# Two attention layers: where the compression weights are loaded and split, the order of the stick-breaking projections, and how small vectors reach 128 partitions

## The chip, the cores and the metric

The kernel runs on one core of one Trainium2 chip. The metric is the device time of one execution in microseconds. The engines are named as the profile names them: PE is TensorE, DVE is VectorE, ACT is ScalarE, POOL is GpSimd, SP is SyncE, which here only issues transfers. PEclk is TensorE's granted clock as a share of the full 2.4 GHz.

## What is computed

A sequence of 256 tokens of width 1024 goes through a first block and then through two hybrid layers. Each of them is a feed-forward part, a mixer and another feed-forward part. The first block's mixer has forgetting attention and differential attention; the hybrid mixer has three branches. Cut to what touches the change:

```python
def token_mixer(h, w_in, fox_forget_b, lam_q1, lam_k1, lam_q2, lam_k2, subln_g, w_out, layer):
    proj = h @ w_in
    ...
    log_f = log_sigmoid(fgate + fox_forget_b)
    ...
    lam = exp(sum(lam_q1 * lam_k1)) - exp(sum(lam_q2 * lam_k2)) + lam_init
    diff_o = a1 - lam * a2
    diff_o = rms_norm(diff_o, subln_g) * (1.0 - lam_init)

def hybrid_mixer(h, w_in, w_gate, nsa_q_norm, nsa_k_norm, nsa_cmp_pe, nsa_cmp_w1, nsa_cmp_w2, ...):
    (sb_q, sb_k, sb_v, nq, nkc, nvc, nks, nvs, nkw, nvw, ngate,
     dq, dk, dv, iq, ik, iw) = split(h @ w_in)
    o_a = stick_breaking_attention(sb_q, sb_k, sb_v)          # 4 heads of 64
    o_b = nsa_attention(nq, nkc, nvc, nks, nvs, nkw, nvw, ngate, ...)
    o_c = dsa_attention(dq, dk, dv, iq, ik, iw, dsa_q_norm, dsa_k_norm, ...)
    g_a, g_b, g_c = split(sigmoid(h @ w_gate), 3)
    merged = g_a * (o_a @ w_br_a) + g_b * (o_b @ w_br_b) + g_c * (o_c @ w_br_c)
    return merged @ w_out

def nsa_compress(x, pe, w1, w2):      # w1: 2048 x 128, twice a layer (keys, values)
    ...
    return silu(flat @ w1) @ w2
```

The small vectors are gains of 64 numbers (nsa_q_norm, three of nsa_k_norm, dsa_q_norm, dsa_k_norm), and in the first mixer subln_g (128), the forget bias (8) and four lambda vectors (64 each).

## The kernel before

All products of activations with weights are made in fp32r, in three matmuls each (mm3, lines 250 to 254): a weight tile of 128x1024 numbers is loaded by SP into a buffer raw (fetch, four buffers), ACT copies it to hi (line 238), DVE subtracts to get lo (line 239), and PE multiplies hi with the high part of the activations, lo with the high part, and hi with the low part. The name after the underscore in a row is the section of the program in which the tile was made: ffn, m (first mixer), and in the hybrid mixer sb (stick-breaking projections), ckv (compressed, selected and windowed keys and values), nq (nsa's queries), ix (the index), dsaq (dsa's queries, keys, values), top, cmp (compression), nsa, dsa, gate, br (branch weights), wo.

The program is written section by section; a scheduler then orders the instructions of each engine, and an engine works through its own queue strictly in that order. The queue matters in four places here.

- The stick-breaking projection. self.proj runs 256 value columns, evacuated by ACT as sbv, then 512 columns of queries and keys, evacuated by ACT in two halves as tok_sb (line 512 through scaled), which PE transposes (tp_sb, line 558) before the scores at_sb (line 906). With skew, the first token tile's matmuls start ahead of the second's.
- The small vectors. small_load issues a transfer from POOL's software queue, which reads one vector for all 128 partitions (partition_broadcast, small_gain).
- The compression weights w1. Eight loads of 256 KB (line 1033) are issued behind nq's weight loads into buffers that are free there, and split_w1 makes their hi (line 1098, ACT) and lo (line 1099, DVE), 128x512 at a time. It is called in section cmp, but the scheduler puts the splits among the steps of ix and dsaq.
- The gate's products (mm_gate, 288 matmuls in a layer) need only the normalised activations and their own weights. The scheduler spreads them as filler over dsaq, cmp, nsa and dsa, up to the branch products mm_br.

In dsaq, the evacuated projection is normalised, multiplied by the gain gA and rotated by a chain of small DVE steps (lines 549, 531 to 539, 552, 521 to 524), to tok_dsaq; PE then transposes it (tp_dsaq, line 1084).

Of the kernel before, what the change touches and what calls it, by code (L numbers as in the profile page):

```python
# [117 lines left out]
class K:  # L118
    def __init__(self, ctx, tc, d):
        self.tc, self.nc, self.d = tc, tc.nc, d  # L120
        nc = self.nc
# [128 lines left out]
    def mm3(self, out, xh, xl, wh, wl, first, last):  # L250
# [242 lines left out]
        with self.tc.issue_after(self.lastpow):  # L493
            self.nc.gpsimd.dma_start(out=out, in_=in_)

    def small_gain(self, pool, g, reps, tag):

        n = g.shape[0]
        t = self.tile(pool, [P, reps, n], tag)
        self.small_load(out=t, in_=bass.AP(tensor=g.tensor, offset=g.offset,  # L500
                                                    ap=[[0, P], [0, reps], [1, n]]))
        return t
# [142 lines left out]
    def mixer1(self, nxt):  # L645
        nc, tc, d = self.nc, self.tc, self.d
        self.sec = "m1"
        self.exp_ln_tables()
        xs = self.prenorms(d["mix_pre_g"][0])
        w = d["w_in"][0]  # L650
        with tc.tile_pool(name="mix1", bufs=1) as mp:
            T = lambda shape, tag, bufs=1, dt=F32: self.tile(mp, shape, tag, dt, bufs)
# [32 lines left out]
            with tc.issue_after(self.lastlo):  # L685
                post = self.gain(d["mix_post_g"][0], mp)
                sel = T([96, 8 * P], "sel", 1, BF)
                self.small_load(out=sel, in_=d["const_sel"])
                gsub = self.small_gain(mp, d["diff_subln_g"][0], 4, "gsub")
                nc.vector.tensor_scalar(out=gsub, in0=gsub, scalar1=0.8, scalar2=None, op0=OP.mult)  # L690
                fb = self.small_gain(mp, d["fox_forget_b"][0], 1, "fb")[:, 0]
                lv = T([P, 4, 64], "lv")
# [148 lines left out]
    def mixer2(self, l, nxt):  # L841
# [7 lines left out]
        with ExitStack() as outer:  # L849
# [27 lines left out]
            kn = G("nsa_k_norm")
            gS = T([P, 4, 64], "gS")
            self.small_load(out=gS[:, 0:2], in_=self.rep(kn[1], 2))
            self.small_load(out=gS[:, 2:4], in_=self.rep(kn[2], 2))  # L880
            gC = T([P, 64], "gC")
            self.small_load(out=gC, in_=kn[0].partition_broadcast(P))
            w2 = T([P, 2, 64], "w2")
            self.small_load(out=w2, in_=G("nsa_cmp_w2").rearrange("v h d -> h v d"))
            pe = T([32, P], "pe")
            self.small_load(out=pe, in_=G("nsa_cmp_pe").rearrange("v (m r) d -> (v m) (r d)", r=2))
# [142 lines left out]
            last = T([P, 8, P], "dq")  # L1029
            raws += [last[:, :4], last[:, 4:]]  # L1030
            for i, r in enumerate(raws):
                with tc.issue_after(self.lastraw):
                    nc.sync.dma_start(out=r, in_=G("nsa_cmp_w1")[i // 4, 512 * (i % 4):512 * (i % 4) + 512]
                                      .rearrange("(m p) h -> p m h", p=P))
            homes = [L([P, 4, 2, P], "gl", 6, F32R) for _ in range(6)]
            homes.append(self.tile(self.spool, [P, 4, 2, P], "xg", F32R, bufs=1))
            homes += [T([P, 2, 2, P], "sp", 2, F32R) for _ in range(2)]
            w1 = [u[:, m] for u in homes for m in range(u.shape[1])]

            gA = T([P, 5, 64], "gA")  # L1040
            self.small_load(out=gA[:, 0:4], in_=self.rep(G("dsa_q_norm"), 4))
            self.small_load(out=gA[:, 4:5], in_=self.rep(G("dsa_k_norm"), 1))
# [50 lines left out]
            def split_w1(i):
                for k in range(0, 4, 4 if i < 7 else 2):
                    u = homes[i + k // 2]
                    r = raws[i][:, k:k + u.shape[1]]
                    with tc.issue_after(self.lasthi):
                        nc.scalar.copy(u[:, :, 0], r)
                    nc.vector.tensor_sub(u[:, :, 1], r, u[:, :, 0].bitcast(F32))  # L1099
# [354 lines left out]
```

## Time and profile before

| | |
|---|---|
| time, median of 3 runs | 1785.98 us (1784.88 to 1786.46) |
| the profiled execution's own time | 1785.48 us |
| its span, first to last instruction | 1783.7 us |
| mean granted clock of PE | 0.994 |
| PE, DVE, ACT, POOL busy | 98%, 63%, 52%, 2% of the span |
| chain that ended last, by engine | PE 86%, DVE 7%, ACT 4%, DMA 3%, issue 1% |
| q0 (small vectors, issued by POOL) | 848 packets, 1.48 MB, 1.5% of 16 engines' span |
| q1 (weights, issued by SP) | 150400 packets, 301.61 MB, 54.4% |

All times are of one core. The profile is of one execution, whose own time stands beside its span. Layer 0's mixer begins at about 710 us and layer 1's at about 1339 us, 629 us later, and the two look alike; the first mixer begins at about 204 us.

### The profile page before, as it was taken

The page shows a single profiled execution, that of the slowest core. Times are in us where ns is not written, and L with a number is a line of the kernel's source. Part 1 is how long each engine was busy: PE and PEld are TensorE (multiplying, and loading weights), DVE is VectorE, ACT ScalarE, POOL GpSimd, SP SyncE. Part 2 cuts the span into 40 slices and gives each one's busy share as a digit, 9 for nine tenths or more (in the row PEclk, how much of TensorE's full clock was granted, in tenths as well). Part 3 has the DMA queues.
Part 4 walks back from the last instruction along what each step waited for, and adds up shares of the span by engine and source line. Part 5 has one row for each costly group of instructions (what it writes and reads, how often), then busy time and mean ns, then how long its engine had stood idle before and what let it go on. Part 6 is the DMA issues. An engine that isn't in the chain of part 4 may idle for free.

```text
span 1783.7 us, 22942 instructions
## 1 busy us (share of the span) xinstructions
PE 1743.5 (98%) x8461; PEld 1433.3 (80%) x8461; DVE 1115.8 (63%) x1801; ACT 931.6 (52%) x1445; POOL 44.2 (2%) x81
## 2 busy tenths in 40 slices
PE   8999989999999999989999999999999899999999
PEld 6888777888878888867887888888888777878887
DVE  5555577555565556697867555555555978675553
ACT  5444467544454444666655444444445756554442
POOL 0000200000000000000000000000001000000000
PEclk9999999999999999999999999999999999999999
DMA  8665754466556656734245665566567353356653
GB/s 279 185 187 191 187 144 142 136 185 187 188 172 206 185 184 203 179 117 141 86 129 187 199 184 184 189 194 185 188 205 176 114 147 91 110 165 207 185 187 130
DMA packets 151952, 305.08 MB, mean 171 GB/s; under 512 B 10440, under 2 KB 42224, under 8 KB 151840
## 3 DMA queue, kind: packets, MB, share of 16 engines
q1 hardware_dynamic: 150400, 301.61, 54.4%
q0 software_dynamic: 848, 1.48, 1.5%
q8 instruction: 67, 1.10, 0.3%
q10 hardware_dynamic: 592, 0.53, 0.1%
q14 instruction: 45, 0.37, 0.1%
HBM read 302.53 MB, written 1.05 MB: 170 GB/s over the span
## 4 chain that ended last, share of the span: by engine, by line
PE 86%; DVE 7%; ACT 4%; DMA 3%; issue 1%; POOL 0%; SPq 0%; DVEq 0%; ACTq 0%; POOLq 0%
PE mm_ffn L254 10%; PE mm_ffn L253 10%; PE mm_ffn L252 10%; PE at_ffn L254 9%; PE at_ffn L252 9%; PE at_ffn L253 9%; PE mm_gate L253 2%; PE mm_gate L254 2%; PE mm_gate L252 2%; PE tp_ffn L290 1%; DMA raw_ckv<-in_w_in_dram 1%; PE po_ffn L290 1%; PE mm_m L254 1%; PE mm_m L252 1%; PE mm_m L253 1%
## 5 line engine op out<-in xcount | busy, mean ns | idle before, releaser
L239 DVE TENSOR_TENSOR lo_ffn<-raw_ffn,hi_ffn 128x1024 fp32r<-128x1024 f32 x392 | 478.1, 1225 | 452.9 <-ACT hi_ffn L238 451.7
L238 ACT CAST hi_ffn<-raw_ffn 128x1024 fp32r<-128x1024 f32 x392 | 411.3, 1054 | 498.4 <-PE at_ffn L254 307.3
L252 PE MATMUL mm_ffn<-hi_ffn,xh_ffn 128*128 128x512 f32 x288 | 112.3, 391 | 2.9 <-ACT hi_ffn L345 1.9
L253 PE MATMUL mm_ffn<-lo_ffn,xh_ffn 128*128 128x512 f32 x288 | 112.3, 391 | 1.0 <-DVE lo_ffn L347 1.0
L254 PE MATMUL mm_ffn<-hi_ffn,xl_ffn 128*128 128x512 f32 x288 | 112.2, 390 | 0.0
L253 PE MATMUL mm_ffn<-lo_ffn,ah_ffn 128*128 128x512 f32 x264 | 103.8, 393 | 0.0
L252 PE MATMUL mm_ffn<-hi_ffn,ah_ffn 128*128 128x512 f32 x264 | 103.3, 391 | 0.0
L253 PE MATMUL at_ffn<-lo_ffn,ah_ffn 128*128 128x512 f32 x264 | 103.1, 390 | 0.0
L254 PE MATMUL at_ffn<-hi_ffn,al_ffn 128*128 128x512 f32 x264 | 102.9, 390 | 0.0
L252 PE MATMUL at_ffn<-hi_ffn,ah_ffn 128*128 128x512 f32 x264 | 102.8, 389 | 0.0
L254 PE MATMUL mm_ffn<-hi_ffn,al_ffn 128*128 128x512 f32 x264 | 102.8, 389 | 0.0
L252 PE MATMUL at_ffn<-hi_ffn,xh_ffn 128*128 128x512 f32 x240 | 94.5, 394 | 0.0
L254 PE MATMUL at_ffn<-hi_ffn,xl_ffn 128*128 128x512 f32 x240 | 93.5, 390 | 0.0
L253 PE MATMUL at_ffn<-lo_ffn,xh_ffn 128*128 128x512 f32 x240 | 93.4, 389 | 0.0
L252 PE MATMUL mm_gate<-hi_gate,xh_ffn 128*128 128x512 f32 x192 | 79.3, 415 | 4.6 <-DVE xg_nq L1099 4.6
L253 PE MATMUL mm_gate<-lo_gate,xh_ffn 128*128 128x512 f32 x192 | 80.1, 417 | 1.6 <-DVE lo_gate L239 1.6
L254 PE MATMUL mm_gate<-hi_gate,xl_ffn 128*128 128x512 f32 x192 | 80.6, 420 | 0.0
L253 PE MATMUL mm_ffn<-lo_ffn,xh_wo 128*128 128x512 f32 x192 | 74.9, 390 | 0.0
L254 PE MATMUL mm_ffn<-hi_ffn,xl_wo 128*128 128x512 f32 x192 | 74.8, 389 | 0.0
L252 PE MATMUL mm_ffn<-hi_ffn,xh_wo 128*128 128x512 f32 x192 | 74.7, 389 | 0.0
L252 PEld LDWEIGHTS mm_ffn<-hi_ffn,xh_ffn 128*128 128x128 f32 x288 | 54.1, 188 | 14.9 <-ACT hi_ffn L345 2.6
L253 PEld LDWEIGHTS mm_ffn<-lo_ffn,xh_ffn 128*128 128x128 f32 x288 | 54.1, 188 | 12.7 <-DVE lo_ffn L347 1.6
(624 smaller groups left out, 4003.3 us busy)
## 6 DMA issues: line engine op xcount, KB each, us to landing
raw_ffn<-in_ffn_w_gu_dram SPq DMA_DIRECT2D x160, 512.0 KB, 3.7
raw_ffn<-in_ffn_w_down_dram SPq DMA_DIRECT2D x132, 512.0 KB, 3.2
raw_gate<-in_w_gate_dram SPq DMA_DIRECT2D x48, 512.0 KB, 3.7
raw_ffn<-in_ffn_w_gate_dram SPq DMA_DIRECT2D x40, 512.0 KB, 4.3
raw_ffn<-in_ffn_w_up_dram SPq DMA_DIRECT2D x40, 512.0 KB, 3.7
raw_m<-in_w_in_dram SPq DMA_DIRECT2D x22, 512.0 KB, 4.0
raw_ffn<-in_ffn_w_gu_dram SPq DMA_DIRECT2D x32, 256.0 KB, 3.2
raw_wo<-in_w_out_dram SPq DMA_DIRECT2D x16, 512.0 KB, 3.5
```

Source lines behind the costliest of these rows:

```text
L238: self.lasthi = nc.scalar.copy(hi, raw).ins
L239: self.lastlo = nc.vector.tensor_sub(lo, raw, hi.bitcast(F32)).ins
L252: nc.tensor.matmul(out, xh, wh, start=first, stop=False)
L253: nc.tensor.matmul(out, xh, wl, start=False, stop=False)
L254: self.lastmm = nc.tensor.matmul(out, xl, wh, start=False, stop=last).ins
L290: nc.tensor.transpose(p[:, i], src[:, i * P:(i + 1) * P], self.ident)
```

## The change

It has three parts.

1. The eight loads of w1 are issued right behind the hybrid mixer's first eight weight loads, into buffers ob0, qS and ob1. load and split are called from wtiles: with each weight tile that the projection takes, one more entry of self.extra is run. Seven of the eight splits (now lines 900 and 901) thus stand between the first weight tiles' splits; the eighth stays in cmp.
2. Queries and keys (512 columns, with skew) are projected first, the 256 value columns behind them.
3. The small vectors are loaded to one partition (rows), in a row of the tile junk, and spread by one matmul with a column of -1 into PSUM; ACT copies them out with a scale of -1 (in the first mixer, -0.8 for the gain that DVE scaled before).

```diff
@@ wtiles
             hi, lo = self.load(w, r0 + k0 * P, m, c0, n)
+            if self.extra:
+                self.extra.pop(0)()
             yield k0, [(hi[:, k], lo[:, k]) for k in range(m)]
@@
-    def small_gain(self, pool, g, reps, tag):
...
+    def rows(self, vecs):
+
+        n = sum(v.shape[-1] * (v.shape[0] if len(v.shape) > 1 else 1) for v in vecs)
+        row = self.tile(self.spool, [1, n], "junk", bufs=1)
+        c = 0
+        for v in vecs:
+            v = v if len(v.shape) == 1 else v.rearrange("a b -> (a b)")
+            self.small_load(out=row[:, c:c + v.shape[0]], in_=v[None, :])
+            c += v.shape[0]
+        p = self.tp([P, n])
+        self.nc.tensor.matmul(p, self.neg1[:1].bitcast(F32), row, start=True, stop=True)
+        return p
@@ the first mixer
-                gsub = self.small_gain(mp, d["diff_subln_g"][0], 4, "gsub")
-                nc.vector.tensor_scalar(out=gsub, in0=gsub, scalar1=0.8, scalar2=None, op0=OP.mult)
-                fb = self.small_gain(mp, d["fox_forget_b"][0], 1, "fb")[:, 0]
+                r = self.rows([d["diff_subln_g"][0], d["fox_forget_b"][0]]
+                              + [d["diff_lambda_" + n][0] for n in ("q1", "k1", "q2", "k2")])
+                gsub = T([P, 4, P], "gsub")
+                nc.scalar.activation(gsub, r[:, None, :P].to_broadcast([P, 4, P]), AF.Copy, scale=-0.8)
+                fb = T([P, 8], "fb")
+                self.scaled(fb, r[:, P:P + 8], -1.0)
                 lv = T([P, 4, 64], "lv")
-                for i, n in enumerate(("q1", "k1", "q2", "k2")):
-                    self.small_load(out=lv[:, i], in_=d["diff_lambda_" + n][0].partition_broadcast(P))
+                self.scaled(lv, r[:, P + 8:].rearrange("p (i d) -> p i d", d=64), -1.0)
@@ the hybrid mixer
+            raws = []
+            for u in (L([P, 8, P], "ob0"), T([P, 16, P], "qS"), L([P, 8, P], "ob1")):
+                raws += [u[:, i:i + 4] for i in range(0, u.shape[1], 4)]
...
+            def extra(k):
+                if k < 8:
+                    load_w1(k)
+                if 0 <= k - 3 < 7:
+                    split_w1(k - 3)
+            self.extra = [lambda k=k: extra(k) for k in range(10)]
+
             self.sec = "sb"
-
-            sbv = [T([P, 256], f"sbv{t}") for t in range(2)]
-            self.proj(xs, w, 512, 256, lambda t, ps: self.scaled(sbv[t], ps, xs[t][2]), skew=True)
-            gQ = T([P, 64], "gQ")
-            self.small_load(out=gQ, in_=G("nsa_q_norm").partition_broadcast(P))
...
-            self.proj(xs, w, 0, 512, sb_evac)
+            self.proj(xs, w, 0, 512, sb_evac, skew=True)
+            sbv = [T([P, 256], f"sbv{t}") for t in range(2)]
+            self.proj(xs, w, 512, 256, lambda t, ps: self.scaled(sbv[t], ps, xs[t][2]))
+            r = self.rows([G("nsa_q_norm"), G("nsa_k_norm"), G("dsa_q_norm"), G("dsa_k_norm")])
...
-            raws = [L([P, 8, P], "ob1")]
-            raws = [raws[0][:, :4], raws[0][:, 4:]]
-            raws += [T([P, 4, P], tag, bufs) for tag, bufs in (("rl", 2), ("rl", 2), ("P", 3), ("P", 3))]
...
@@ cmp
             for v in range(2):
-                for i in range(4):
-                    split_w1(4 * v + i)
+                if v == 1:
+                    split_w1(7)
```

The scheduler decides what this does to each engine's queue. The first place is SP's queue at the start of layer 0's mixer, where raw_sb and raw_ckv are loads of mixer weights and raw_nq those of nsa's queries. Before, from the seventh mixer load on, and then at the end of nq's loads:

```order
L223 DMA raw_ckv_6166<-in_w_in_dram 128x2x512
L223 DMA raw_ckv_6184<-in_w_in_dram 128x2x512
L281 DMA gain_wo_8515<-in_ffn_norm_dram 128x1024
L223 DMA raw_ckv_6202<-in_w_in_dram 128x2x512
...
L223 DMA raw_nq_6481<-in_w_in_dram 128x2x512
L223 DMA raw_nq_6499<-in_w_in_dram 128x2x512
L1033 DMA ob_nq_6579<-in_nsa_cmp_w_2_dram 128x4x128 x2
L1033 DMA dq_nq_6584<-in_nsa_cmp_w_2_dram 128x4x128 x2
L1033 DMA P_nq_6582<-in_nsa_cmp_w_2_dram 128x4x128
L223 DMA raw_ix_6610<-in_w_in_dram 128x3x296
L1033 DMA P_nq_6583<-in_nsa_cmp_w_2_dram 128x4x128
```

Now, from the same load on:

```order
L224 DMA raw_ckv_6202<-in_w_in_dram 128x2x512
L224 DMA raw_ckv_6223<-in_w_in_dram 128x2x512
L891 DMA ob_pn_5876<-in_nsa_cmp_w_2_dram 128x4x128 x2
L891 DMA qS_pn_5877<-in_nsa_cmp_w_2_dram 128x4x128 x4
L891 DMA ob_pn_5878<-in_nsa_cmp_w_2_dram 128x4x128 x2
L284 DMA gain_wo_8523<-in_ffn_norm_dram 128x1024
L224 DMA raw_ckv_6244<-in_w_in_dram 128x2x512
L224 DMA raw_ckv_6264<-in_w_in_dram 128x2x512
```

The eight loads of nsa_cmp_w1 have moved ahead of gain_wo and of the third raw_ckv.

The second place is ACT's queue in the same stretch; L238 (now L239) makes hi of a weight tile, tok_sb are the evacuated queries and keys. Before:

```order
L238 CAST hi_sb_6007<-raw_sb_6005 128x1024
L238 CAST hi_ckv_6168<-raw_ckv_6166 128x1024
L238 CAST hi_ckv_6186<-raw_ckv_6184 128x1024
L238 CAST hi_ckv_6204<-raw_ckv_6202 128x1024
L512 ACTIVATE tok_sb_6023<-mm_sb_5949,rsv_pn_5866 128x256
L512 ACTIVATE tok_sb_6023<-mm_sb_5949,rs_ffn_5780 128x256
L512 ACTIVATE tok_sb_6032<-mm_sb_5950,rsv_pn_5866 128x256
```

Now, from the first split of w1 (L900) on:

```order
L294 CAST xh_ffn_5839<-po_ffn_5850 128x512
L900 CAST gl_pn_5879<-ob_pn_5876 128x4x128
L520 ACTIVATE tok_sb_5967<-mm_sb_5887,rsv_pn_5871 128x256
L520 ACTIVATE tok_sb_5967<-mm_sb_5887,rs_ffn_5785 128x256
L239 CAST hi_sb_5991<-raw_sb_5989 128x1024
L900 CAST gl_pn_5880<-ob_pn_5876 128x4x128
L239 CAST hi_sb_6024<-raw_sb_6022 128x1024
L900 CAST gl_pn_5881<-qS_pn_5877 128x4x128
L239 CAST hi_ckv_6204<-raw_ckv_6202 128x1024
L900 CAST gl_pn_5882<-qS_pn_5877 128x4x128
L520 ACTIVATE tok_sb_5976<-mm_sb_5888,rsv_pn_5871 128x256
L520 ACTIVATE tok_sb_5976<-mm_sb_5888,rs_ffn_5860 128x256
```

tok_sb stood behind the third hi_ckv; it stands behind hi_sb of the value weights now, with three splits of w1 around it, and the third hi_ckv behind all of it.

The third place is the end of dsaq in layer 0. On DVE, where gl and xg are homes of the split w1, L549 (now L557) begins tok_dsaq and lo_gate is the low part of a gate weight tile. Before:

```order
L1099 TENSOR_TENSOR gl_nq_6595<-rl_nq_6580,gl_nq_6595 128x4x128
L1062 COPY zs_ix_6606<-tp_ix_6704 128x128
L1099 TENSOR_TENSOR gl_nq_6596<-rl_nq_6581,gl_nq_6596 128x4x128
L1099 TENSOR_TENSOR gl_nq_6597<-P_nq_6582,gl_nq_6597 128x4x128
L549 SCALAR_TENSOR_TENSOR tok_dsaq_6789<-mm_dsaq_6715,rs_ffn_5780,gA_nq_6602 128x320
L531 TENSOR_REDUCE sm_dsaq_6793<-junk_dsaq_6790 128x5
L1099 TENSOR_TENSOR gl_nq_6598<-P_nq_6583,gl_nq_6598 128x4x128
L1099 TENSOR_TENSOR xg_nq_6599<-dq_nq_6584,xg_nq_6599 128x4x128
```

Now:

```order
L1088 COPY zs_ix_6626<-tp_ix_6707 128x128
L901 TENSOR_TENSOR sp_cmp_6999<-ob_pn_5878,sp_cmp_6999 128x2x128
L901 TENSOR_TENSOR sp_cmp_7000<-ob_pn_5878,sp_cmp_7000 128x2x128
L240 TENSOR_TENSOR lo_gate_7712<-raw_gate_7709,hi_gate_7711 128x1024
L1088 COPY zs_ix_6626<-tp_ix_6724 128x128
L557 SCALAR_TENSOR_TENSOR tok_dsaq_6809<-mm_dsaq_6735,rs_ffn_5785,gA_sb_6070 128x320
L539 TENSOR_REDUCE sm_dsaq_6813<-junk_dsaq_6810 128x5
L240 TENSOR_TENSOR lo_gate_7730<-raw_gate_7727,hi_gate_7729 128x1024
```

The splits of w1, but for the last, are gone from here, and the first lo_gate stands ahead of tok_dsaq. On PE, at the same place, behind the last product of dsaq. Before:

```order
L254 MATMUL mm_dsaq_6716<-hi_dsaq_6773,xl_ffn_5835 128x408
L252 MATMUL mm_gate_7699<-hi_gate_7703,xh_ffn_5759 128x512
L252 MATMUL mm_gate_7700<-hi_gate_7703,xh_ffn_5834 128x512
L1084 MATMUL tp_dsaq_6814<-ident,tok_dsaq_6789 128x128 x2
L1084 MATMUL tp_dsaq_6814<-ident,kd_dsaq_6812 128x128
L253 MATMUL mm_gate_7699<-lo_gate_7704,xh_ffn_5759 128x512
```

Now:

```order
L257 MATMUL mm_dsaq_6736<-hi_dsaq_6793,xl_ffn_5840 128x408
L255 MATMUL mm_gate_7707<-hi_gate_7711,xh_ffn_5764 128x512
L256 MATMUL mm_gate_7707<-lo_gate_7712,xh_ffn_5764 128x512
L257 MATMUL mm_gate_7707<-hi_gate_7711,xl_ffn_5765 128x512
...
L256 MATMUL mm_gate_7708<-lo_gate_7730,xh_ffn_5839 128x512
L257 MATMUL mm_gate_7708<-hi_gate_7729,xl_ffn_5840 128x512
L1110 MATMUL tp_dsaq_6834<-ident,tok_dsaq_6809 128x128 x2
```

Two gate matmuls stood between the last mm_dsaq and the first tp_dsaq; 24 stand there now (rows 3458 to 3481 of PE's order).

## Rows read from the trace of the kernel before

**Rows 1.** Page, part 1: busy us (share of the span) x instructions, by engine.

```profile
PE 1743.5 (98%) x8461; PEld 1433.3 (80%) x8461; DVE 1115.8 (63%) x1801; ACT 931.6 (52%) x1445; POOL 44.2 (2%) x81
```

**Rows 2.** Waits of PE: line <- engine and line waited for: us in total, times, longest.

```profile
PE tp_dsaq L1084 <- DVE tok_dsaq L524: 4.8, 2, 2.4
PE mm_gate L252 <- DVE xg_nq L1099: 4.6, 2, 2.3
PE tp_sb L558 <- ACT tok_sb L512: 3.8, 2, 2.1
PE tp_m L662 <- ACT hi_m L238: 2.9, 1, 2.9
...
PE mm_gate L253 <- DVE lo_gate L239: 1.6, 2, 0.8
```

**Rows 3.** Timeline, start of layer 0's mixer: start us, us, engine, line, [idle before <-releaser].

```profile
726.14 0.39 PE L254 MATMUL mm_sb<-hi_sb,xl_ffn 128*128 128x512 f32 x1
...
726.82 0.39 PE L254 MATMUL mm_sb<-hi_sb,xl_ffn 128*128 128x512 f32 x1
727.42 1.04 ACT L238 CAST hi_ckv<-raw_ckv 128x1024 fp32r<-128x1024 f32 x1 [4.52 <-DMA raw_ckv<-in_w_in_dram]
...
728.89 0.80 PE L558 MATMUL tp_sb<-ident,tok_sb 128*128 128x128 f32 x4 [1.68 <-ACT tok_sb L512]
```

**Rows 4.** Chain that ended last, first mixer and layer 0's mixer: start us, us, what.

```profile
212.50 10.00 DMA raw_m<-in_w_in_dram
...
717.28 10.04 DMA raw_ckv<-in_w_in_dram
```

**Rows 5.** DMA queues over 708 to 730: packets, MB, share of 16 engines' time.

```profile
q1 hardware_dynamic: 2034, 3.30, 41.1%
q0 software_dynamic: 272, 0.44, 39.6%
```

**Rows 6.** The same over 205 to 230, first mixer.

```profile
q0 software_dynamic: 304, 0.59, 34.9%
```

**Rows 7.** Windows: length, busy us of each engine (x), granted clock, DMA share, GB/s.

```profile
225.80:230.00 4.20, 4.20 (x16) 3.47 (x17) 3.09 (x7) 1.74 (x3) 0.00 (x0) 0.59 0.88 274
712.00:727.00 15.00, 15.00 (x85) 12.97 (x82) 6.31 (x8) 5.82 (x8) 5.38 (x9) 1.00 0.85 131
783.00:795.00 12.00, 6.89 (x34) 5.33 (x32) 11.89 (x40) 9.22 (x23) 0.00 (x0) 0.92 0.02 6
795.40:800.00 4.60, 4.60 (x11) 3.64 (x12) 4.48 (x12) 0.63 (x2) 0.00 (x0) 0.50 0.47 121
800.00:906.00 106.00, 105.29 (x608) 85.08 (x606) 84.31 (x234) 69.70 (x165) 0.62 (x2) 1.00 0.38 110
1424.50:1428.00 3.50, 3.50 (x8) 2.82 (x9) 3.38 (x11) 0.63 (x2) 0.00 (x0) 0.50 0.49 150
1440.00:1446.00 6.00, 6.00 (x22) 4.64 (x23) 4.45 (x18) 4.36 (x8) 0.00 (x0) 0.72 0.39 114
```

**Rows 8.** Timeline, end of dsaq in layer 0, columns as in group 3.

```profile
787.97 0.39 PE L252 MATMUL mm_gate<-hi_gate,xh_ffn 128*128 128x512 f32 x1
788.48 0.54 DVE L549 SCALAR_TENSOR_TENSOR tok_dsaq<-mm_dsaq,rs_ffn,gA_nq 128x320 f32<-128x320 f32 x1
...
793.55 0.69 PE L1084 MATMUL tp_dsaq<-ident,tok_dsaq 128*128 128x128 f32 x2 [2.40 <-DVE tok_dsaq L524]
...
794.13 1.22 DVE L239 TENSOR_TENSOR lo_gate<-raw_gate,hi_gate 128x1024 fp32r<-128x1024 f32 x1
```

**Rows 9.** Groups by line: shapes xcount | busy us, mean ns of one | idle before.

```profile
L1099 DVE TENSOR_TENSOR gl_nq<-ob_nq,gl_nq 128x512 fp32r<-128x512 f32 x4 | 2.7, 685 | 0.0
...
L1098 ACT CAST gl_nq<-ob_nq 128x512 fp32r<-128x512 f32 x4 | 2.5, 613 | 0.0
...
L906 PE MATMUL at_sb<-sT_sb 64*128 64x256 f32 x8 | 2.3, 402 | 0.0
...
L512 ACT ACTIVATE sbv_sb<-mm_sb,rs_ffn 128x256 f32<-128x256 f32 x4 | 1.9, 476 | 2.2 <-PE mm_sb L254 2.2
```

More of the change, by code (lines that the diff above doesn't have):

```diff
@@ L134, in __init__ @@
         self.first_gate = self.zeros = None
+        self.extra = []
         self.x = []
@@ L494, in small_load @@
             self.nc.gpsimd.dma_start(out=out, in_=in_)
-    def small_gain(self, pool, g, reps, tag):
[L498 to L502, printed above, removed]
+    def rows(self, vecs):
[9 more added lines that the diff above has]
+        return p
     def proj(self, xs, w, c0, n, evac, mk=None, skew=False):
@@ L869, in mixer2 @@
             lp = mp
-            self.sec = "sb"
-            sbv = [T([P, 256], f"sbv{t}") for t in range(2)]
-            self.proj(xs, w, 512, 256, lambda t, ps: self.scaled(sbv[t], ps, xs[t][2]), skew=True)
-            gQ = T([P, 64], "gQ")
-            self.small_load(out=gQ, in_=G("nsa_q_norm").partition_broadcast(P))
[L877 to L886, printed above, removed]
+            raws = []
+            for u in (L([P, 8, P], "ob0"), T([P, 16, P], "qS"), L([P, 8, P], "ob1")):
+                raws += [u[:, i:i + 4] for i in range(0, u.shape[1], 4)]
@@ new lines, in mixer2, with load_w1, split_w1 @@
+            homes = [L([P, 4, 2, P], "gl", 6, F32R) for _ in range(6)]
+            homes.append(self.tile(self.spool, [P, 4, 2, P], "xg", F32R, bufs=1))
+            w1 = [u[:, m] for u in homes for m in range(4)]
+            def load_w1(i):
+                with tc.issue_after(self.lastraw):
+                    nc.sync.dma_start(out=raws[i], in_=G("nsa_cmp_w1")[i // 4, 512 * (i % 4):512 * (i % 4) + 512]
+                                      .rearrange("(m p) h -> p m h", p=P))
+            def split_w1(i):
+                us = homes[i:i + 1] if i < 7 else [T([P, 2, 2, P], "sp", 2, F32R) for _ in range(2)]
+                for j, u in enumerate(us):
+                    n = 4 // len(us)
+                    r = raws[i][:, n * j:n * j + n]
+                    with tc.issue_after(self.lasthi):
+                        nc.scalar.copy(u[:, :, 0], r)
+                    nc.vector.tensor_sub(u[:, :, 1], r, u[:, :, 0].bitcast(F32))
+                    if i == 7:
+                        w1.extend(u[:, m] for m in range(n))
@@ L894, in sb_evac @@
                 self.transposes([tok[:, i * P:(i + 1) * P] for i in range(4)], sT[:, :, toks[t]])
-            self.proj(xs, w, 0, 512, sb_evac)
+            self.proj(xs, w, 0, 512, sb_evac, skew=True)
+            sbv = [T([P, 256], f"sbv{t}") for t in range(2)]
+            self.proj(xs, w, 512, 256, lambda t, ps: self.scaled(sbv[t], ps, xs[t][2]))
+            r = self.rows([G("nsa_q_norm"), G("nsa_k_norm"), G("dsa_q_norm"), G("dsa_k_norm")])
+            r = r.rearrange("p (i d) -> p i d", d=64)
+            gQ = T([P, 64], "gQ")
+            self.scaled(gQ, r[:, 0], -1.0)
+            gC = T([P, 64], "gC")
+            self.scaled(gC, r[:, 1], -1.0)
+            gS = T([P, 2, 2, 64], "gS")
+            self.scaled(gS, r[:, 2:4, None, :].to_broadcast([P, 2, 2, 64]), -1.0)
+            gS = gS.rearrange("p a b d -> p (a b) d")
+            gA = T([P, 5, 64], "gA")
+            self.scaled(gA[:, 0:4], r[:, 4:5].to_broadcast([P, 4, 64]), -1.0)
+            self.scaled(gA[:, 4], r[:, 5], -1.0)
+            w2 = T([P, 2, 64], "w2")
+            self.small_load(out=w2, in_=G("nsa_cmp_w2").rearrange("v h d -> h v d"))
+            pe = T([32, P], "pe")
+            self.small_load(out=pe, in_=G("nsa_cmp_pe").rearrange("v (m r) d -> (v m) (r d)", r=2))
             oa = [L([P, 256], f"oa{t}") for t in range(2)]
@@ L1023, in mixer2 @@
             self.proj(xs, w, 768, 512, nq_evac)
-            raws = [L([P, 8, P], "ob1")]
-            raws = [raws[0][:, :4], raws[0][:, 4:]]
-            raws += [T([P, 4, P], tag, bufs) for tag, bufs in (("rl", 2), ("rl", 2), ("P", 3), ("P", 3))]
[L1029 to L1042, printed above, removed]
             self.sec = "ix"
@@ L1091, in mixer2 @@
             after = self.lastT
[L1093 to L1099, printed above, removed]
             self.sec = "top"
```

## The prediction

> **What bounds the kernel now.** The page's busy times come first: TensorE (PE) is busy 1743.5 of 1783.7 us [rows 1]. What the change can give is therefore about 40 us of PE idle time, and whatever is lost at a low clock. The view of waits says who ends that idle time [rows 2]. Two waits at the end of the section dsaq lead it: 4.8 us for DVE's tok_dsaq and 4.6 us for DVE's xg_nq of line 1099, each in two pieces, one for each layer, and with them goes 1.6 us for lo_gate. Then come 3.8 us for ACT's tok_sb at the start of the two hybrid mixers, and 2.9 us for ACT's hi_m in the first mixer.
>
> I then looked at what is late in each place. At the hybrid mixer's start ACT idles 4.52 us at hi_ckv until a transfer raw_ckv lands; tok_sb stands behind it in ACT's queue, and PE idles 1.68 us for that [rows 3]. This raw_ckv took 10.04 us from issue to landing, and the raw_m that holds the first mixer 10.00 us [rows 4]. The DMA view says what the engines did meanwhile: over 22 us the software queue q0, which carries the small vectors, moved 0.44 MB and took 39.6% of 16 engines, 8.7 us, while q1 moved 3.30 MB in 41.1%, 9.0 us [rows 5]. In the first mixer q0 took 34.9% of 25 us, again 8.7 us, for 0.59 MB [rows 6]. At the end of dsaq nothing is late but DVE itself: from 783 to 795 it is busy 11.89 of 12 us while PE does 6.89 [rows 7], because splits of the compression weights (L1099) stand ahead of the steps of tok_dsaq and of lo_gate, which starts only at 794.13 [rows 8].
>
> After the first mixer's stall, and after those of dsaq, the granted clock falls: 0.59 over 225.8 to 230, 0.50 over 795.4 to 800 and over 1424.5 to 1428 [rows 7]. That is the lower of the two levels, 1.2 GHz, for all or most of the stretch.
>
> **The change part by part.**
>
> *Compression weights.* In each layer eight loads of 256 KB leave their place behind raw_nq and come behind the mixer's first eight weight loads; seven of the eight splits leave the queues of DVE and ACT at dsaq. A split takes DVE 685 ns and ACT 613 [rows 9]; seven are 4.8 us of DVE. In the orders lo_gate now stands ahead of tok_dsaq, so PE has 24 gate matmuls before the transposes tp_dsaq, where it had two; matmuls of 512 columns follow each other by 0.227 us (0.68 over three) [rows 3], so 24 last 5.4 us. They can begin at 787.97, where the first one stands now [rows 8], and end at 793.4. The chain of tok_dsaq now takes 5.1 us, from 788.48 until the transposes begin at 793.55 [rows 8], with two whole w1 splits and half a one in it, 1.8 us; in the new order two lo_gate splits, 2.4 us by their 1.2 us of spacing, take that place, and the chain can begin a us sooner, since no split stands ahead of it: about 5.7 us from 787.4, or 793.1. I take the whole wait as gone: 4.6 + 4.8 + 1.6 = **11.0 us**. The bound below is that half of it comes back as a later wait.
>
> These gate matmuls come from the end. Counted in the orders, 250 stand between the first tp_dsaq and the last po_dsa before, 260 after, so the attention steps keep their filler; behind po_dsa 4 remain instead of 36, ahead of the branch weights' matmuls (mm_br), which need no result of po_dsa in their first twelve.
>
> The new place has room: from 712 to 727 DVE is busy 6.31 of 15 us and ACT 5.82 [rows 7], and 4.8 and 4.3 us are added. The loads, 2 MB, take 5.7 us at the rate of q1 above (3.30 MB in 9.0 us). Issued from about 711, when their places come free, they are in by 717, and ACT reaches the first split at about 720. I price all this at nothing; its cover is the idle share, and without it each split costs its 0.6 to 0.7 us.
>
> *Queries and keys first.* The 512 columns run first now, the 256 value columns after: the same matmuls, so no cost. But tok_sb stands behind the value weights' hi_sb and the first hi_ckv, not behind the third, the late one, and that one is wanted by PE some 9 us later than before. So both layers' waits go, even with a transfer that stays late: **3.8 us**.
>
> *Small vectors.* Four loads to one partition (six in the first mixer) replace the spread ones, and queue on POOL as those did. The old ones moved pieces of 256 bytes: 0.44 MB are some 1,700, so 8.7 us x 16 engines / 1,700 = 80 ns of an engine each. In the hybrid mixer 80 KB of w2 and pe remain, 320 pieces, and 64 tiny ones: 1.9 us instead of 8.7. In the first mixer the rows of sel remain, 96, and some 96 tiny pieces; 304 packets there were some 1,250 pieces, so the rest is 1.3 us if a piece has the price, 192 of 304 or 5.5 us if a packet has it. raw_m must land 2.9 us sooner for PE not to wait; by pieces it gains 7.4, by packets 3.2. The wait goes either way: **2.9 us**.
>
> New work: a matmul of one row against 384 columns in full fp32, three times in all. The nearest row is at_sb, 64x256 in that type, 402 ns [rows 9], or 600 ns for 384 columns. The bound below is the 0.227 us per 512 columns of the split matmuls, 0.17. I take the row of the same type: **+1.8 us** in all. The Trainium skill (TensorE: Matmul & The Clock Gate, "Why this matters for your kernels") says that a matmul over few rows takes as long as one over all 128; no run here shows it yet, and by it too one row gets no discount against the 64 of at_sb.
>
> Then come three to five ACT copies, mostly of up to 256 columns, at 476 ns [rows 9]: 1.4 us in the first mixer, 2.4 in each hybrid one, 6.2 us if all lay on the path, 0 if PE's other matmuls cover them. In the first mixer DVE now waits for one of them (lv) with the softmax's steps queued behind it, but PE's order has some 19 value matmuls there. Nearer cover than exposure: I take 0.5 us a mixer, **+1.5 us**.
>
> *Clock.* If the stalls go, so does the fall behind them: 4.20 x 0.41 = 1.7, 4.60 x 0.50 = 2.3, 3.50 x 0.50 = 1.75: **5.8 us**. Below, nothing: the clock also fell, to 0.72, over 1440 to 1446, with PE busy throughout [rows 7].
>
> **Sum.** 11.0 + 3.8 + 2.9 + 5.8 - 1.8 - 1.5 = 20.2 us. The profiled execution took 1785.48 (its span is 1783.7), 0.5 under the median of the runs, 1785.98: so 1765.3 against the one, **1766 us** against the other, 1.1% less. Under 0.2% (3.6 us) a change can't be told from none here.
>
> **The rivals.**
>
> *The small vectors are not what holds raw_m.* Then the first mixer keeps its 2.9 us and the 1.7 us of clock behind it, while the hybrid starts, which gain by the order, change alike: 1766 + 4.6 = **1771 us**. For it: the lateness is inferred from shares of engines that both queues use; against it, q0's 8.7 us in both places [rows 5, 6]. The Trainium skill (DMA: Bandwidth & Descriptors, "Why small descriptors are slow (HBM only)") would side with this rival: it puts the overhead of a 256-byte descriptor at 27%, by which q0's 0.44 MB should take an estimated 1.5 us at q1's rate; the row has 8.7, so the trace disagrees.
>
> *DVE's chain becomes the bound between dsaq and po_dsa.* Over 800 to 906 PE is busy 105.29 of 106 us, DVE 84.31 [rows 7], in steps that wait for each other. If that chain sets the pace and not PE, what lo_gate and the clock give there is lost in new waits: 1.6 + 2.3 + 1.75 = 5.7, **1771 to 1772 us**. Against it: DVE carries two lo_gate splits less behind tp_dsaq, PE ten gate matmuls more.
>
> *Slower: the 2 MB hold ACT's queue.* The splits stand in strict order ahead of tok_sb and of weight splits. The landing has about 3 us to spare (717 against 720), and weights split ahead some 5 more; each us beyond is a us of PE in each layer. At 10 us beyond, the 20 us are eaten: that takes 18 us beyond the 5.7 that 2 MB need. At 20 us, 2 x 2 us more, **1790 us**. The worst landings in the trace are 10 us late [rows 4], in the crowd that the change thins. A light form, 5 us in each layer, gives 1776.
>
> **How the numbers follow.** My forecast 0.62; late raw_m 0.14; DVE's chain 0.11; the light form of the held queue 0.04; the gain eaten up to nothing 0.05; slower 0.04. So faster 0.91, same 0.05, slower 0.04. Upwards the range takes in the two middle rivals and most of both at once, 1775; downwards the 3.3 us of costs at zero, the fall at 1440 gone too (6 x 0.28 = 1.7), and a us or two of other waits: 1759.
>
> **What would show it.** Right: no PE wait over 0.5 us for tok_dsaq, xg_nq, tok_sb or hi_m; clock 1.00 behind the three places; q0 under 3 us of 16 engines; the splits of L900 and L901 in idle time at the mixer's start. Wrong: new PE waits for P_sb or sT_sb in the stick-breaking part, for P_nsa in the attention steps, or at mm_br; ACT waiting for a transfer at L900.

## The result and the profile after

| | before | after |
|---|---|---|
| time, median of 4 runs each | 1785.58 us | 1761.37 us (1760.33 to 1764.53) |
| ratio, 95% interval | | 0.9867 [0.985, 0.9884] |
| the profiled execution's own time, span | 1785.48, 1783.7 us | 1760.33, 1758.3 us |
| mean granted clock of PE | 0.994 | 1.000 |

The forecast was 1766 us, 20 us less; measured are 24 us less by the medians and 25.4 us by the spans of the two profiled executions. The page of the changed kernel (span, busy times, and of part 3 the software queue):

```profile
span 1758.3 us, 22921 instructions
...
PE 1735.1 (99%) x8461; PEld 1428.5 (81%) x8467; DVE 1113.9 (63%) x1800; ACT 934.3 (53%) x1458; POOL 40.1 (2%) x77
...
q0 software_dynamic: 640, 0.37, 0.1%
```

PE's busy time fell by 8 us, though it has more to do: at a granted clock of 0.50 a matmul of 512 columns lasted 0.63 us (796 to 799 of before), at 1.00 it lasts 0.39, and up to the last microsecond this profile has none left at the low clock. q0's packets moved 0.37 MB instead of 1.48. The waits of PE, in the form of [rows 2], now begin with these:

```profile
PE mm_wo L255 <- ACT xh_br L294: 1.5, 2, 0.7
PE tp_ffn L293 <- DVE xg_ffn L305: 1.4, 4, 0.5
PE mm_ffn L164 <- DVE gain_ffn L160: 1.3, 1, 1.3
...
PE tp_dsaq L1110 <- DVE tok_dsaq L532: 0.2, 1, 0.2
```

The first three stood in the old list too, behind the five shown in [rows 2]. Of those five only tok_dsaq is left, once and with 0.2 us. Two small ones are new, 0.5 us for kd_cmp in each layer and 0.3 to 0.4 us for qS_nq, three times in all. The stretches of [rows 7], moved to where the same work stands now (226 to 230, 712 to 727, 789.4 to 794, 794 to 900, 1408.9 to 1412.4, 1424 to 1430):

```profile
226.00:230.00 4.00, 4.00 (x19) 3.34 (x18) 3.09 (x4) 2.52 (x3) 0.00 (x0) 1.00 0.45 120
712.00:727.00 15.00, 14.98 (x93) 12.81 (x92) 11.30 (x14) 12.17 (x23) 0.10 (x1) 1.00 0.76 235
789.40:794.00 4.60, 4.47 (x21) 3.34 (x20) 4.45 (x13) 2.30 (x5) 0.00 (x0) 1.00 0.77 221
794.00:900.00 106.00, 104.71 (x610) 85.12 (x611) 83.77 (x234) 70.14 (x167) 0.62 (x2) 1.00 0.39 110
1408.90:1412.40 3.50, 3.50 (x17) 2.90 (x16) 3.38 (x10) 1.92 (x4) 0.00 (x0) 1.00 0.80 210
1424.00:1430.00 6.00, 6.00 (x42) 5.23 (x39) 5.14 (x20) 5.20 (x9) 0.00 (x0) 1.00 0.32 89
```

The third column from the end is the granted clock: 1.00 everywhere, also in the last stretch, which answers to 1440 to 1446 of before. From 712 to 727 DVE and ACT do about twice what they did, and PE works through it. At the end of dsaq (columns as in [rows 3]):

```profile
780.08 1.22 DVE L240 TENSOR_TENSOR lo_gate<-raw_gate,hi_gate 128x1024 fp32r<-128x1024 f32 x1
...
781.45 0.55 DVE L557 SCALAR_TENSOR_TENSOR tok_dsaq<-mm_dsaq,rs_ffn,gA_sb 128x320 f32<-128x320 f32 x1
...
787.55 0.39 PE L1110 MATMUL tp_dsaq<-ident,tok_dsaq 128*128 128x128 f32 x2
```

lo_gate starts before tok_dsaq's chain, and the transposes follow the 24 gate matmuls, with the 0.2 us of wait that the list above has. In the forecast the chain took 5.7 us; from 781.45 to 787.55 it is 6.1. The DMA view, over 705 to 735 (layer 0's start) and then over 205 to 230, against [rows 5, 6]:

```profile
q0 software_dynamic: 192, 0.08, 1.0%
...
raw_ckv<-in_w_in_dram SPq DMA_DIRECT2D x4, 512.0 KB, 4.5
...
qS_pn<-in_nsa_cmp_w_dram SPq DMA_DIRECT2D x4, 256.0 KB, 4.5
```

```profile
q0 software_dynamic: 256, 0.20, 2.4%
...
raw_m<-in_w_in_dram SPq DMA_DIRECT2D x6, 512.0 KB, 4.6
```

q0 is down to 0.3 us of 16 engines in the one (1.0% of 30 us) and 0.6 in the other, where before had 8.7 in each, and the weights land after 4.5 and 4.6 us where the same views of before have 8.6 and 9.3 (medians). Where the 25.4 us lie is read from the start times of the same instruction in the two timelines, the first or last of a tile; the forecast's terms are sorted into the same places:

| stretch | forecast | measured |
|---|---|---|
| before the first mixer (nothing changed there) | 0 | -0.8 |
| first mixer, last po_ffn to last po_m | -2.9 - 1.7 + 0.6 + 0.5 = -3.5 | -3.8 |
| both hybrid mixers, first mm_sb to last mm_dsaq | -3.8 + 2 x (0.6 + 0.5) = -1.6 | -1.4 - 1.5 = -2.9 |
| last mm_dsaq to last po_wo, both layers | -11.0 - 4.1 = -15.1 | -8.1 - 9.6 = -17.7 |

The first row is chance: PE's wait for the first hi_ffn is 1.9 us in the profile of before, none is listed in that of the changed kernel, and in the other runs it is 0.4 to 2.0 us.

### The profile page after: what moved, and what is told of

Same layout as the page of the kernel before. It is cut to its first block, busy times and chain, and to the rows that moved or that the text cites. A ratio compares the mean times of both kernels' runs of the same rounds, so it can differ in the third digit from the quotient of the medians.

```text
span 1758.3 us, 22921 instructions
## 1 busy us (share of the span) xinstructions
PE 1735.1 (99%) x8461; PEld 1428.5 (81%) x8467; DVE 1113.9 (63%) x1800; ACT 934.3 (53%) x1458; POOL 40.1 (2%) x77
## 4 chain that ended last, share of the span: by engine, by line
PE 89%; DVE 6%; ACT 3%; issue 1%; DMA 1%; POOL 0%; SPq 0%; DVEq 0%; ACTq 0%; POOLq 0%
PE mm_ffn L257 11%; PE mm_ffn L256 11%; PE mm_ffn L255 11%; PE at_ffn L257 9%; PE at_ffn L255 9%; PE at_ffn L256 9%; PE mm_gate L256 2%; PE mm_gate L257 2%; PE mm_gate L255 2%; PE tp_ffn L293 1%; PE po_ffn L293 1%; PE mm_m L257 1%; PE mm_m L255 1%; PE mm_m L256 1%; PE at_top L1133 1%
## 5 line engine op out<-in xcount | busy, mean ns | idle before, releaser
L239 ACT CAST hi_ffn<-raw_ffn 128x1024 fp32r<-128x1024 f32 x392 | 411.1, 1054 | 498.5 <-PE at_ffn L257 307.6
L257 PE MATMUL mm_gate<-hi_gate,xl_ffn 128*128 128x512 f32 x192 | 77.0, 404 | 0.0
L256 PEld LDWEIGHTS mm_ffn<-lo_ffn,xh_ffn 128*128 128x128 f32 x288 | 54.1, 188 | 12.7 <-DVE lo_ffn L350 1.6
```

Of the source, the lines that this page charges most:

```text
L239: self.lasthi = nc.scalar.copy(hi, raw).ins
L256: nc.tensor.matmul(out, xh, wl, start=False, stop=False)
L257: self.lastmm = nc.tensor.matmul(out, xl, wh, start=False, stop=last).ins
```

## The experiments

Each ratio is to the kernel before measured beside that run. Its medians there were 1786.89 to 1787.54 us, against 1785.58 beside the changed kernel, so medians of runs that were not measured together can differ by 2 us for that alone.

The theory: each of the three parts gives its term of the sum, the early compression weights most of it. Its rivals: the weights' place gives little without a light queue; the order of the projections, not the queue, frees the hybrid starts; the slow pieces are slow for another reason than their size.

**e1_w1_old.** The changed kernel with w1's loads behind nq and its splits called in cmp, as before.

```diff
-            self.extra = [lambda k=k: extra(k) for k in range(10)]
...
             self.proj(xs, w, 768, 512, nq_evac)
+            raws = [L([P, 8, P], "ob1")]
+            ...
+            for i, r in enumerate(raws):
+                with tc.issue_after(self.lastraw):
+                    nc.sync.dma_start(out=r, in_=G("nsa_cmp_w1")...)
```

> The changed kernel with the compression weights loaded and split where they were before; vectors and stick-breaking order as changed. Theory: their place is worth what the two ends of dsaq lost, by the two profiles 8.3 us in layer 0 and 9.3 in layer 1: 1779 us, with the PE waits for tok_dsaq and xg_nq back at about 2.3 us each and the granted clock near 0.5 for some 4 us behind them. Rival: the gain came from the lighter software queue and the order of the projections, and the gate matmuls fill dsaq anyway: 1763 to 1766 us.

1782.04 us, ratio to before 0.9977 [0.9968, 0.9987]. PE's waits at dsaq's end are 5.4, 5.2 and 4.7 us (lo_gate, tok_dsaq, sm_dsaq), 7.6 us in each layer, where before had 5.5: the scheduler's order there is not quite that of before. The theory's sign holds and its 1779 is 3 us short: from the last mm_dsaq to the last po_wo the two layers take 2.9 and 1.2 us longer than in before. e11 below takes the same part alone, with before's order.

**e2_vec_old and e4_vec_distinct.** All small vectors spread by the software queue again; in e4 each partition reads another row of a weight matrix.

```diff
-            r = self.rows([G("nsa_q_norm"), G("nsa_k_norm"), G("dsa_q_norm"), G("dsa_k_norm")])
...
+            self.small_load(out=gQ, in_=G("nsa_q_norm").partition_broadcast(P))
```
```diff
+    def spread(self, w, n, reps, j):
+        return bass.AP(tensor=w.tensor, offset=w.offset + 512 * j, ap=[[w.shape[1], P], [n, reps], [1, n]])
...
-            self.small_load(out=gQ, in_=G("nsa_q_norm").partition_broadcast(P))
+            self.small_load(out=gQ, in_=self.spread(G("w_gate"), 64, 1, 0))
```

> The changed kernel with all small vectors spread by the software queue again, as before, in both kinds of mixer. Theory: q0 again holds raw_m, so the first mixer's wait of 2.9 us for hi_m and its clock fall come back (+3.9 us by the two profiles), while the hybrid mixers' starts stay free of waits by their order: 1765 us. Rival, that the small vectors never held the weight loads: 1761 us.

> As e2 (spread loads, the same number of pieces, each of the same size), but each of the 128 partitions reads its piece from a different row of a weight matrix instead of all from one address, so the gains are other numbers. If a piece of 256 bytes has the price (80 ns of an engine), q0 takes about 8.7 us of 16 engines in each mixer as before, and the time is that of e2, 1765 us. If reading one address again and again has the price, q0 takes about 1.5 us by the 0.29 us that 320 pieces of other loads took in the changed kernel, raw_m is in time, and the time is 1761 to 1762 us.

e2 took 1769.50 us (0.9902 [0.9889, 0.9916]), e4 1756.79 (0.983 [0.9816, 0.9843]). The two differ in addresses alone, and by 12.7 us. The DMA views over 205 to 230, first e2, then e4:

```profile
q0 software_dynamic: 304, 0.59, 36.7%
...
raw_m<-in_w_in_dram SPq DMA_DIRECT2D x6, 512.0 KB, 9.7
```

```profile
q0 software_dynamic: 304, 0.59, 7.9%
...
raw_m<-in_w_in_dram SPq DMA_DIRECT2D x6, 512.0 KB, 4.6
```

The same 304 packets and 0.59 MB take 9.2 us of 16 engines from one address for each vector, and 2.0 us from 128 addresses; raw_m lands after 9.7 and after 4.6 us. Over 705 to 735 it is the same, e2 first:

```profile
q0 software_dynamic: 272, 0.44, 18.5%
...
raw_ckv<-in_w_in_dram SPq DMA_DIRECT2D x6, 512.0 KB, 10.0
```

```profile
q0 software_dynamic: 272, 0.44, 4.4%
...
raw_ckv<-in_w_in_dram SPq DMA_DIRECT2D x4, 512.0 KB, 4.3
```

So neither the pieces' size nor their number has the price, but that all of them read one address: e4's 1,700 pieces cost 12 ns of an engine each (4.4% of 30 us x 16 / 1,700). The forecast's 80 ns was worked out rightly and put down to the wrong thing. e4 also reads another tensor, a weight matrix; no run separates that from the addresses. e2 also says that the order of the projections does not free the starts when the transfer stays late. Its waits of PE:

```profile
PE at_sb L976 <- ACT rl_sb L969: 4.2, 2, 2.1
PE mm_ckv L255 <- ACT sbv_sb L528: 3.2, 2, 2.2
PE tp_m L678 <- ACT hi_m L239: 2.9, 1, 2.9
```

The wait for tok_sb is gone, but PE now waits for rl_sb and sbv_sb, which stand in ACT's queue behind the late hi_ckv. My 1765 for e2 was 4.5 us short because of that.

**e3_sb_old.** The value columns first, as before, with the rest of the change.

```diff
+            sbv = [T([P, 256], f"sbv{t}") for t in range(2)]
+            self.proj(xs, w, 512, 256, lambda t, ps: self.scaled(sbv[t], ps, xs[t][2]), skew=True)
...
-            self.proj(xs, w, 0, 512, sb_evac, skew=True)
-            sbv = [T([P, 256], f"sbv{t}") for t in range(2)]
-            self.proj(xs, w, 512, 256, lambda t, ps: self.scaled(sbv[t], ps, xs[t][2]))
+            self.proj(xs, w, 0, 512, sb_evac)
```

> The changed kernel with the 256 value columns projected first again. If the order is what removed the wait for tok_sb at the hybrid mixers' starts, it comes back: 3.8 us, 1765 us. If the lighter software queue suffices, because the third raw_ckv is then no longer late: 1761 to 1762 us. I expect the second.

1763.08 us (0.9865 [0.9851, 0.9878]), not to be told from the changed kernel; no wait for tok_sb is listed. So with the light queue the order is not needed to remove it (e11 shows the same with the compression weights where they were).

**e8_w1_only.** The early compression weights alone, e2 and e3 together.

> The kernel before with the first part of the change alone: the compression weights at the mixer's start; values projected first, vectors spread by the software queue. Theory: dsaq's ends gain all that they gain in the changed kernel, 17.6 to 20 us, and the starts keep their waits: 3.9 us in the first mixer and, as the 2 MB now share the engines with the slow pieces, at least the 4 us that e2 lost in the hybrid starts: 1769 to 1772 us. Rival, that the early loads only pay with the lighter queue: above 1778 us.

1781.07 us (0.9964 [0.9951, 0.9976]): the rival. PE's waits, and the DMA view over 705 to 735:

```profile
PE tp_sb L574 <- ACT tok_sb L528: 13.7, 2, 7.7
PE tp_m L678 <- ACT hi_m L239: 2.9, 1, 2.9
```

```profile
q0 software_dynamic: 272, 0.44, 21.2%
...
raw_ckv<-in_w_in_dram SPq DMA_DIRECT2D x6, 512.0 KB, 14.1
```

The ends of dsaq gain what the theory said (first mm_gate to first mm_br, against before: 9.2 and 10.3 us less), but the starts lose 7.9 and 6.4 us: with 2 MB more to move beside the slow pieces, raw_ckv lands after 14.1 us, tok_sb behind it holds PE for up to 7.7 us, and the granted clock falls behind both stalls (0.53 over 732.5 to 739.7 and over 1360.5 to 1367.8). This is the rival that I had as slower, at a smaller size than it needed.

**e6_norep.** No rows; each vector spread from its address once, its copies made by views.

```diff
-            r = self.rows([G("nsa_q_norm"), G("nsa_k_norm"), G("dsa_q_norm"), G("dsa_k_norm")])
...
+            gK = T([P, 3, 64], "gS")
+            kn = G("nsa_k_norm")
+            self.small_load(out=gK, in_=bass.AP(tensor=kn.tensor, offset=kn.offset, ap=[[0, P], [64, 3], [1, 64]]))
...
             gA = T([P, 5, 64], "gA")
...
+            self.small_load(out=gA[:, 3], in_=G("dsa_q_norm").partition_broadcast(P))
+            self.small_load(out=gA[:, 4], in_=G("dsa_k_norm").partition_broadcast(P))
+            nc.gpsimd.tensor_copy(gA[:, 0:3], gA[:, 3:4].to_broadcast([P, 3, 64]))
```

> The changed kernel without rows: the small vectors are again spread from one address to 128 partitions by the software queue, but each vector once (a subln gain and no four copies of it; nsa_k_norm's three in one piece of 768 bytes), the copies made by views and one POOL copy. Pieces of one address fall from 1408 to 512 in a hybrid mixer, from 1152 to 768 in the first. If the price is by the piece, q0 takes about 2.6 us of 16 engines in a hybrid mixer beside the 0.3 us of w2 and pe, the weights are in time there, the row matmuls and their ACT copies are saved, and the first mixer keeps a part of its wait: 1758 to 1760 us. If it is by the 256 bytes, 3.8 us and much the same. If the number of packets holds the queue, it stays near e2's 1769 us.

1756.47 us (0.9824 [0.9811, 0.9837]), faster than both kernels: its interval lies clear of the changed kernel's. It is below the 1758 to 1760 expected, as the first mixer kept no wait. q0 over 705 to 735, and over 205 to 230:

```profile
q0 software_dynamic: 208, 0.28, 5.3%
...
raw_ckv<-in_w_in_dram SPq DMA_DIRECT2D x4, 512.0 KB, 4.6
```

```profile
q0 software_dynamic: 256, 0.40, 15.0%
...
raw_m<-in_w_in_dram SPq DMA_DIRECT2D x6, 512.0 KB, 4.5
```

1.6 and 3.8 us of 16 engines are little enough for the weights to land in time, and the matmuls of one row with their ACT copies are saved. By the spans (1758.3 and 1754.8) these cost 3.5 us, by the medians 4.9. From the last po_ffn before the first mixer to the last po_wo the two timelines differ by 4.9 us too; the spans have less because e6 lost 1.3 us ahead of that, where the two kernels are the same.

**e10_norep_sb_old and e11_norep_only.** e6 with the value columns first; then the same with w1's loads and splits as before too, which leaves the single spreading as the only change to the kernel before.

> e6 with the 256 value columns projected first, as before. If the light queue alone keeps the weights in time, as e3 showed with rows, the order is worth nothing: 1756 to 1758 us. If the 1.3 us that the pieces of one address still take in e6 make the third raw_ckv late enough, the wait for tok_sb comes back: 1759 us and more.

> The kernel before with the small vectors alone spread once each, as in e6; compression weights and order as before. Theory: the waits at the mixers' starts go (2.9 and 3.8 us) with the first clock fall (1.7): 1777 to 1779 us; dsaq's waits and clock falls stay. Rival, that the starts only gain with the new order of the projections: 1781 to 1782 us, from the first mixer alone.

e10 took 1760.08 us (0.9852 [0.9837, 0.9868]), e11 1776.73 (0.9946 [0.9934, 0.9959]). e11 was met: the starts' waits are gone, and dsaq's are those of [rows 2]:

```profile
PE tp_dsaq L1102 <- DVE tok_dsaq L532: 4.8, 2, 2.4
PE mm_gate L255 <- DVE xg_nq L1060: 4.6, 2, 2.3
PE mm_gate L256 <- DVE lo_gate L240: 1.6, 2, 0.8
```

The two ran side by side, and their difference, 16.7 us, is the place of the compression weights by itself; the stretch from the first mm_sb to the last mm_dsaq, where they are now split, is only 0.2 and 0.1 us longer for it. e10 came out as neither of its two expectations: it has no wait for tok_sb, yet e6's order is 3.6 us better by the medians, with intervals that just touch; in the two timelines the stretch from the first mm_sb to the last mm_dsaq is 0.9 us shorter in each layer with queries and keys first. So the three parts, in e6's form, give 10.2 (vectors), 16.7 (weights) and about 3 us (order).

**e7_dummy and e9_dummy36.** The kernel before with 24 or 36 idle matmuls ahead of dsaq's transposes.

```diff
                 p = self.tp([P, 3, P])
+                for i in range(24 if t == 0 else 0):
+                    nc.tensor.matmul(p, xs[0][0][:, 0], xs[0][0][:, 0:3], start=True, stop=True)
```

> The kernel before, with 24 matmuls of 384 columns into the transposes' PSUM tile ahead of the two gate matmuls at the end of dsaq, in each layer; nothing reads them. They fill some 4 of the 5.5 us in which PE idles there and take no work off DVE. If the fall of the clock behind dsaq comes from PE's idling, the clock stays at 1.00 over 795 to 800 and 1424 to 1428, and the time falls by about 4 us, to 1782 us (5.7 with the fall at 1440). If it falls for another reason, the clock and the time stay, 1786 us.

> As e7, with 36 idle matmuls instead of 24 at each end of dsaq; they last 6.5 us and cover the second wait too, at the price of up to a us by which the transposes come late. e7 left 1.8 us of idle time in layer 0 and the clock fell there a little later, while in layer 1 it did not fall. If the fall follows PE's idling, the clock now stays at 1.00 in both layers from the end of dsaq to the branch products; if not, layer 0 falls again to about 0.5 for some 4 us. The time of the whole moves by less than can be told, 1784 to 1788 us.

e7 took 1786.71 us (0.9996 [0.9986, 1.0005]), e9 1783.68 (0.9982 [0.9973, 0.9991]). The windows of e7 at the ends of dsaq:

```profile
794.00:798.00 4.00, 2.11 (x10) 1.15 (x9) 3.94 (x18) 1.50 (x7) 0.00 (x0) 1.00 0.00 0
798.00:802.00 4.00, 4.00 (x12) 3.12 (x11) 3.91 (x10) 1.23 (x3) 0.00 (x0) 0.57 0.61 144
1425.00:1429.00 4.00, 2.10 (x9) 1.14 (x8) 3.94 (x18) 1.50 (x6) 0.00 (x0) 1.00 0.00 0
1429.00:1433.00 4.00, 3.72 (x17) 2.55 (x16) 3.91 (x11) 1.34 (x3) 0.00 (x0) 1.00 0.58 142
```

and of e9, with the stretch at 809.5:

```profile
787.00:797.00 10.00, 9.75 (x54) 9.06 (x53) 9.89 (x36) 6.12 (x17) 0.00 (x0) 1.00 0.04 4
797.00:802.00 5.00, 4.72 (x22) 3.33 (x21) 4.83 (x12) 1.68 (x3) 0.00 (x0) 1.00 0.60 199
809.50:816.60 7.10, 7.10 (x23) 5.45 (x22) 4.84 (x19) 4.01 (x9) 0.00 (x0) 0.54 0.35 109
1419.00:1430.00 11.00, 10.76 (x59) 9.76 (x57) 10.88 (x39) 6.13 (x18) 0.00 (x0) 1.00 0.11 35
```

In e7 PE still idles 1.9 us of 4 in both layers; the clock falls in layer 0 (0.57 over 798 to 802) and not in layer 1. The expected 1782 us did not come. From the last mm_dsaq to the last po_wo e7 wins 0.3 us in layer 0 and 2.5 in layer 1, and it loses more in places that it doesn't touch: 0.6 and 2.1 us at the hybrid starts, where the wait for tok_sb was 0.7 and 0.6 us longer and in layer 1 a fall followed it (0.72 over 1360 to 1366), and 1.6 us in the first mixer (0.57 over 224 to 232, where before has 0.79).

In e9 PE idles next to nothing, and the clock stays at 1.00 behind dsaq, up to 802 in layer 0 and throughout in layer 1. But layer 0 has a new fall at 809.5 to 816.6 (0.54) with PE busy throughout, so the expectation, 1.00 up to the branch products, was met in layer 1 alone. The clock of every execution says more than the one profile: e9's ten have 0.996 to 1.000 as their means, the fifteen of before beside them 0.992 to 0.995, and e9's two at 1.000 took 1779.73 and 1780.25 us, where before's median is 1786.89. So with PE's idling taken away and DVE's work left as it was, most of the low clock goes: the fall behind dsaq follows PE's idling, though not each fall does.

## Why the prediction was right

**Compression weights.** The mechanism was as described and the term carried the result. The 11.0 us of waits and the clock behind them came to 17.7 us where the sum had 15.1. Of the 2.6 us more, 1.7 are the fall at 1440 to 1446 [rows 7], which isn't in the changed kernel's profile and which the sum left out, as a fall with no wait before it. The place taken alone is worth 16.7 us (e10 against e11). That it was free at the mixer's start was right only with a light queue (0.1 to 0.2 us a layer, e10 against e11): e8 shows the cost without it, 14 us of the 20.

**Queries and keys first.** The step that failed is "So both layers' waits go, even with a transfer that stays late". The term's size, 3.8 us, came out, but by the light queue (e3, e11); with a late transfer the wait moves on to rl_sb and sbv_sb (e2). Between e10 and e6 the order has a gain of its own, 0.9 us a layer, that the forecast did not have. Between e3 and the changed kernel it is 0.1 us in layer 0, and 1.7 in layer 1, where e3's clock fell; so with the rows in place that gain isn't shown, and why the hybrid starts gave 2.9 us instead of 1.6, though the new work cost more, stays open.

**Small vectors.** That they held raw_m and raw_ckv is shown by e4 against e2, so the first rival falls. The price by the piece was wrong in its cause: 320 pieces of w2 and pe were to keep 1.6 us and take about 0.3; they come from different addresses. In e4 the 0.44 MB took 1.3 us, and in before 8.7, for the one address; the forecast had taken the 8.7 for the price of small pieces. The Trainium skill (DMA: Bandwidth & Descriptors, "Why small descriptors are slow (HBM only)") puts the overhead of a 256-byte descriptor at 27%, from which the prediction had an estimate of 1.5 us. e4 comes near it, but as near to the 1.2 us that 0.44 MB take at q1's rate [rows 5] without any overhead, so the 27% itself is not shown here.

**New work.** The three matmuls of one row were put at 0.60 us each. In the changed kernel's timeline, where the program's one matmul stands as two, with the copies behind:

```profile
723.61 0.91 PE L509 MATMUL tp_sb<-junk_sb,neg 1*128 1x384 f32 x2
...
724.45 1.57 PE L951 MATMUL at_sb<-sT_sb 64*128 64x256 f32 x8
725.03 0.23 ACT L520 ACTIVATE gQ_sb<-tp_sb 128x64 f32<-128x64 f32 x1
725.14 0.22 ACT L520 ACTIVATE gC_sb<-tp_sb 128x64 f32<-128x64 f32 x1
...
725.25 0.39 ACT L520 ACTIVATE gS_sb<-tp_sb 128x256 f32<-128x256 f32 x1
```

PE is held for 0.84 us, from 723.61 to 724.45, so the three cost an estimated 2.5 us instead of 1.8. The row taken for the price was no good neighbour: at the pace of at_sb's eight matmuls here, 1.57 us for 8 x 256 columns, 384 columns would take 0.3 us, and why one row takes longer no run shows. Of the copies one takes ACT 0.22 to 0.23 us for 64 columns and 0.39 for 256, some 1.5 us in a hybrid mixer, partly covered. In all 3.5 to 4.9 us where the sum had 3.3.

**DVE's chain as the bound.** It did not come: over 794 to 900 PE is busy 104.71 of 106 us, and no wait between dsaq and mm_br is longer than the 0.5 us for kd_cmp, which is new.

**Left open.** Falls of the clock that follow no wait of a microsecond or more: 1440 to 1446 in before, 809.5 to 816.6 in e9, 804 to 808 and 1432 to 1436 in e11, 241 to 245 and 1347 to 1351 in e3, in one profiled execution each. They cost 1.7 to 3.3 us apiece (6 x 0.28, 7.1 x 0.46), come at different places, and stand in kernels with early and with late splits; the changed kernel's profile has none, nor have those of e4 and e6. That is the changed kernel's profile, though, not the kernel: its four executions have mean clocks of 1.000, 0.999, 0.997 and 0.999 and took 1760.33, 1761.83, 1764.53 and 1760.91 us, and the profile is of the first. A thousandth of 1760 us is 1.8 us, about one such fall, so the others had some. No run settled what sets them off, and so a part of the 25.4 us by the spans, and of the 2.6 us that the ends of dsaq gave beyond the forecast, is luck of the one execution.

## What to carry to other kernels

Ask of a slow transfer not only how many pieces it has but where they are read: beside vectors spread to 128 partitions from one address, weights landed after 9.7 us instead of 4.6, and after 14.1 with 2 MB more under way; spreading each vector once (copies by views) cost less here than a detour over TensorE. Take work off a queue where an engine stands still because of it, but look first whether the new place is quiet in fact: the early weights gave 17 us with a light queue and 6 without. When a stall is taken away, count the low clock behind it too, here a third of the 17 us.

## What was not expected of the hardware

The same 0.59 MB in the same 304 packets took 9.2 us of 16 engines from one address a vector and 2.0 us from many (e2, e4). And the clock fell to 0.54 over 7 us in which PE was busy throughout (e9), where before kept 1.00 at the same work, over 800 to 906 [rows 7]. Matmuls that compute nothing, put where PE had idled, raised the mean clock of an execution from between 0.992 and 0.995 to between 0.996 and 1.000 (e9), and the two at 1.000 were some 7 us shorter.
